# A hybrid retention and attention block on one core: six units in the lead, and rotary units written out by hand before the values

## The chip, the cores and the metric

The kernel runs on one core of a Trainium2 chip, in one launch, and computes the whole block for 256 tokens. The metric is the device time of one execution in microseconds (us). For the kernel before there are three runs, of 1586.11, 1587.36 and 1590.63 us, and one profiled execution of 1590.42 us.

## What is computed

The input `x` has 256 tokens of width 2048. The part of the reference that the change touches is the projection of the tokens and what becomes of queries, keys and values of the retention branch:

```python
proj = u @ w_in                      # u = rmsnorm(x); w_in is 2048 x 11328
(r_q, r_k, r_v, r_g, c_q, c_kv, k_pe, g_ret, g_mla) = split(proj)
rq = rope(r_q as 8 heads of 128, positions)
rk = rope(r_k as 8 heads of 128, positions) * 128 ** -0.5
rv = r_v as 8 heads of 256
ry = groupnorm(retention(rq, rk, rv)) * silu(r_g)
merged = sigmoid(g_ret) * (ry @ w_ret_o) + sigmoid(g_mla) * (attention @ w_mla_o)
h = x + merged @ w_out;  h = h + relu(rmsnorm(h) @ w_up) ** 2 @ w_down
```

`rope(t)` gives `t * cos + swapped(t) * sin`, where the two halves of a head change places in `swapped` and `sin` carries the sign. All of it is in float32.

## The kernel before

**Precision.** Every product of float32 numbers is made from two parts, a high part and a low part (`hi`, `lo`). `split` (lines 543 to 551) makes them: ScalarE copies the value into `hi`, and VectorE subtracts to get `lo`. A weight block of 128x1024 numbers therefore costs one ScalarE cast (line 167 or 545) and one VectorE subtraction (line 168 or 546) before TensorE can use it.

**The buffers.** Weights land in `raw` tiles (a ring of five, 4 KB per partition each), and their parts go into rings of four `hi` and four `lo` tiles (`wtile`, lines 158 to 161). TensorE sums into eight banks: four in the pool `mm` and four in the pool `at`. All large tensors share six places of 16 KB per partition (`big`).

**Units.** Queries and keys are made in 16 units of 128 output channels, query and key of a head in turn. A unit takes 16 matmuls of 512 columns and 16 of 256 columns. Units 0 to 2 are made while `x` arrives: the lead (lines 582 to 615) loads blocks that hold 256 columns of transposed `x` and 3x128 weight columns for each of 16 steps of the contracted dimension, into three large tiles and with ten transfers of 316, 384, 640 and then mostly 1280 columns. Units 3 to 5 follow, with their own weight loads, beside the angle tables for the rotation (`angles`, `table`) and the mean square of `x` (`load_x`). Then a loop (lines 709 to 719) makes units 6 to 15; in each turn it joins the unit's two partial sums into an SBUF tile (`join`, lines 533 to 536) and rotates it (`rope`, lines 698 to 707: two multiplications on 64 partitions each, one on 128, and one addition), and until unit 11 it also rotates one early unit. At units 8 and 10 it makes combinations of `x` (`combine`, lines 222 to 237), with two `raw` tiles as working space.

**Products.** The values, and later the gate `gr`, the output product `yr` and the gate `gm`, go through `product` (lines 451 to 481). Each has two column halves of eight steps. Most steps are an `Eight` (two parts of 12 matmuls of 512 columns). In some, the `Seven`, seven products stand for eight; such a step has four parts of 6, 6, 6 and 3 matmuls, and its weights must first be combined on VectorE (lines 302, 311, 312). `SEVEN` says at which of the eight places they stand. A `Seven` uses seven banks, an `Eight` four. The four banks of the `Eight` lie in the pool `mm` in the first half and in `at` in the second, so the first `Seven` of a half needs banks that the half ahead of it still holds until its results have been read (`tokens`, line 725, and `gated`, on VectorE).

**Order.** Most of the kernel is put in order by a scheduler that works from a simulated timeline. The products stand in blocks with an order written by hand (`run`, `stream`, lines 425 to 449): part n is multiplied after the parts up to n+4 have been prepared and those up to n+6 loaded, and a list `later` holds work that is to follow some parts on. Instructions that the scheduler places may stand between those written by hand.

Of the kernel before, what the change touches and what calls it, by code (L numbers as in the profile page):

```python
# [25 lines left out]
RH = 8  # L26
# [34 lines left out]
N_VEC = 60  # L61
LEAD = S + 3 * P
LEAD_TILES = (0, 6, 12)
LEAD_CHUNKS = (0, 1, 2, 4, 6, 8, 10, 12, 14, 16)
C_ID, C_MASK = 0, 128
# [39 lines left out]
def block_kernel(ctx: ExitStack, tc: tile.TileContext, A):  # L105
# [86 lines left out]

    def lora_pair(src, x):
        hi, lo = weights(src, [P, 2, LT, P])
        ps = mmps(f"lt{uid[0]}")
        for i in range(2):
            out = ps[:, i * S : (i + 1) * S]
            for k in range(LT):
                PE.matmul(out, hi[:, i, k], x.hi(k), start=k == 0, stop=False)
                PE.matmul(out, hi[:, i, k], x.lo(k), start=False, stop=False)  # L200
            for k in range(LT):
                PE.matmul(out, lo[:, i, k], x.hi(k), start=False, stop=k == LT - 1)
            yield i, out

# [16 lines left out]

    def combine(pair, j, o):
        n = o.shape[1]
        x, q = wtile("raw", [P, n, 2, 2, P]), wtile("raw", [P, n, 4, P])
# [12 lines left out]
        yield  # L237
        split(o[:, :, 0], o[:, :, 1], q)
# [136 lines left out]
    class Eight:  # L375
# [33 lines left out]
        def after(self, part):  # L409
            pass  # L410
# [170 lines left out]

    lead = [act.tile([P, 4096], F32, tag="act16", name=f"lead{i}") for i in range(3)]
    vec0 = lead[0][:, :N_VEC]
    x = Pair("x")
    posi = ip.tile([P, S], I32, name="posi")
    firsts = [mmps(f"first{j}") for j in range(3)]

    def lead_at(k):
        i = sum(k >= b for b in LEAD_TILES[1:])
        return lead[i], (N_VEC if i == 0 else 0) + (k - LEAD_TILES[i]) * LEAD  # L590

    def lead_x(k):
        t, o = lead_at(k)
        return t[:, o : o + S]

    for k0, k1 in zip(LEAD_CHUNKS, LEAD_CHUNKS[1:]):
        n = k1 - k0
        t, o = lead_at(k0)
        d = N_VEC + k0 * LEAD
        skip = N_VEC if k0 == 0 else 0  # L600
        cuts = (-skip, S, LEAD) if k0 == 0 else (0, n * LEAD)
        for c0, c1 in zip(cuts, cuts[1:]):
            tc.keep_in_program_order(
                nc.sync.dma_start(t[:, o + c0 : o + c1], A["lead"][:, d + c0 : d + c1])
            )
        blk = t[:, o : o + n * LEAD].rearrange("p (k c) -> p k c", c=LEAD)
        for k in range(k0, k1):
            split(x.hi(k), x.lo(k), lead_x(k), scale=vec0[:, V_MIX + k : V_MIX + k + 1])
        hi, lo = (wtile(kind, [P, n, 3 * P]) for kind in ("hi", "lo"))
        split(hi, lo, blk[:, :, S:])  # L610
        for j, ps in enumerate(firsts):
            w = hi[:, :, j * P : (j + 1) * P], lo[:, :, j * P : (j + 1) * P]
            t_pass1(ps, w, x, k0, n, k0 == 0)
            t_pass2(ps, w, x, k0, n, k1 == KT)

# [17 lines left out]

    early = ip.tile([P, 6, S], F32, name="early")
    for j in range(3):
        join(early[:, j], firsts[j])
    con = cp.tile([P, N_CONST], F32, name="con")
    tc.keep_in_program_order(nc.sync.dma_start(con, A["con"]))
    ident = con[:, C_ID : C_ID + P]
    mask = con[:, C_MASK : C_MASK + 384]  # L640

# [3 lines left out]

    firsts.append(mmps("first3"))
    t_half(firsts[3], A["w_rqk"][3], x, 0)
    t_half(firsts[3], A["w_rqk"][3], x, 1)
    tc.keep_in_program_order(nc.sync.dma_start(posi, A["positions"].partition_broadcast(P)))
    V.tensor_copy(posf, posi)  # L650
    join(early[:, 3], firsts[3])
    angles(0)
    xn = ip.tile([P, 2, D], F32, name="xn")
    ssx = ip.tile([P, 2], F32, name="ssx")

    def load_x(t):
        tc.keep_in_program_order(nc.sync.dma_start(xn[:, t], A["x"][t * P : (t + 1) * P]))
        SC.activation(xn[:, t], xn[:, t], AF.Square, accum_out=ssx[:, t : t + 1])

    load_x(0)  # L660
    lates = mmps("first4")
    t_unit(lates, A["w_rqk"][4], x)
    join(early[:, 4], lates)
    load_x(1)
    angles(1)
    lates = mmps("first5")
    t_unit(lates, A["w_rqk"][5], x)
    join(early[:, 5], lates)
    rx = cp.tile([P, 2], F32, name="rx")
# [29 lines left out]
    def rope(out, ps, cos, sin, step):  # L699
        tmp = rope_pool.tile([P, S], F32, tag="rope", name="rope")  # L700
        for d in range(0, P, step):
            s = d + step if (d // step) % 2 == 0 else d - step
            V.tensor_tensor(
                out=tmp[d : d + step], in0=ps[s : s + step], in1=sin[s : s + step], op=ALU.mult
            )
        V.tensor_tensor(out=out, in0=ps, in1=cos, op=ALU.mult)  # L706
        V.tensor_tensor(out=out, in0=out, in1=tmp, op=ALU.add)

    qk = big("qk", shape=(P, 2, RH, S))
    for u in range(6, 2 * RH):  # L710
        if u in (8, 10):
            for _ in combine(x, u - 8, xc[:, u - 8 : u - 6 if u == 8 else 3]):
                pass
        ps = mmps(f"qk{u}")
        t_unit(ps, A["w_rqk"][u], x)
        if u < 12:
            rope(qk[:, u % 2, u // 2 - 3], early[:, u - 6], *tabs[0], 64)
        rope(qk[:, u % 2, u // 2], joined(ps), *tabs[0], 64)
    ictx.close()

    rv = big("rv", shape=(P, 2, D))
    def tokens(out, act):
# [149 lines left out]
    def after(n):  # L872
        nonlocal making
        if n == 20:
            making = combine(ry, 0, yc[:, :2])
        elif n == 32 and yc.shape[1] > 2:
            making = combine(ry, 2, yc[:, 2:])
        if n % 2 == 0:
            next(making, None)
# [4 lines left out]
    with ExitStack() as mctx:  # L884
# [5 lines left out]
        def lora_norm(s, parts):  # L890
            n = len(parts) // 2
            cn = lpool.tile([P, 2, LORA], F32, name=f"cn{s}")
            ss = lpool.tile([P, 2, n], F32, name=f"ss{s}")
            for i, (t, c0, ps) in enumerate(parts):
# [3 lines left out]
                )  # L898
            r = lpool.tile([P, 2], F32, name=f"rc{s}")
            if n == 1:  # L900
# [38 lines left out]
        def late_turn():  # L939
            for _ in lora_turn(1, cn):  # L940
                pass
            pk = atps("pk")
            for t in range(2):
                PE.transpose(pk[:, t * P : (t + 1) * P], kn[:, t].rearrange("p j n -> p (j n)"), ident)
            rope(kpe, pk[:, :S], *tabs[1], 32)

# [31 lines left out]
        def mla_scores(h):  # L978
# [8 lines left out]
            pr = mp.tile([P, 384], F32, tag="pr", bufs=3, name=f"pr{h}")  # L987
            mx = mp.tile([P, 4], F32, tag="mx", bufs=4, name=f"mx{h}")
            parts = (slice(0, P), slice(P, 384))
# [44 lines left out]
        def mla_projections(g):  # L1034
            j0 = 2 * (g % 2)
            for i, ps in lora_pair(A["w_qpe"][g // 2, :, j0 : j0 + 2], cq):
                pe = mp.tile([P, S], F32, tag="pe", bufs=3, name=f"pe{g}{i}")
                rope(pe, ps, *tabs[1], 32)
                pes = vkp[:, 5 + g % 2, i * S : (i + 1) * S].rearrange("p (j n) -> p j n", j=2)
                split(pes[:, 0], pes[:, 1], pe[:, P:])  # L1040
                heads[2 * g + i, "pe"] = pe, pes
                yield
# [497 lines left out]
```

## Time and profile before

| | us |
|---|---|
| median of three runs | 1587.36 |
| the profiled execution | 1590.42 |
| its span, first to last instruction | 1588.7 |
| TensorE busy in the span | 1568.5 |
| VectorE busy | 1307.8 |
| ScalarE busy | 953.9 |

The span is what the views below divide up. The execution's own time is 1.7 us longer than the span. A matmul counts as busy from its start until its modelled end, and matmuls overlap, so a busy TensorE is not yet one at its peak; the distance between the starts of two matmuls says how fast it goes. The granted clock is given as a share of full speed: 1.00 is 2.4 GHz, and the other level, 0.50, is 1.2 GHz.

### The profile page before, as it was taken

The page shows a single profiled execution, that of the slowest core. Times are in us where ns is not written, and L with a number is a line of the kernel's source. Part 1 is how long each engine was busy: PE and PEld are TensorE (multiplying, and loading weights), DVE is VectorE, ACT ScalarE, POOL GpSimd, SP SyncE. Part 2 cuts the span into 40 slices and gives each one's busy share as a digit, 9 for nine tenths or more (in the row PEclk, how much of TensorE's full clock was granted, in tenths as well). Part 3 has the DMA queues.
Part 4 walks back from the last instruction along what each step waited for, and adds up shares of the span by engine and source line. Part 5 has one row for each costly group of instructions (what it writes and reads, how often), then busy time and mean ns, then how long its engine had stood idle before and what let it go on. Part 6 is the DMA issues. An engine that isn't in the chain of part 4 may idle for free.

```text
span 1588.7 us, 21686 instructions
## 1 busy us (share of the span) xinstructions
PE 1568.5 (99%) x7831; PEld 1326.2 (83%) x7831; DVE 1307.8 (82%) x1797; ACT 953.9 (60%) x1398; POOL 40.8 (3%) x75
## 2 busy tenths in 40 slices
PE   8999999999999999999999999999999999999997
PEld 7878888887888889888888888888888888888886
DVE  7999777798976988774667598888877899999996
ACT  6546555465545557765345576666676766666664
POOL 0000000000000000000000000000010100000000
PEclk9999999999999999999999999999999999999999
DMA  8566654455656664444564666667576977686773
GB/s 319 178 208 204 214 174 161 157 196 189 211 164 222 208 202 133 133 133 142 188 227 157 237 236 214 211 230 239 200 234 208 356 268 248 239 311 223 263 254 113
DMA packets 107195, 333.72 MB, mean 210 GB/s; under 512 B 11216, under 2 KB 11856, under 8 KB 106064
## 3 DMA queue, kind: packets, MB, share of 16 engines
q1 hardware_dynamic: 103776, 318.71, 59.8%
q0 software_dynamic: 3168, 11.54, 1.8%
q10 hardware_dynamic: 144, 2.10, 0.4%
q8 instruction: 61, 1.00, 0.3%
q14 instruction: 46, 0.38, 0.1%
HBM read 319.72 MB, written 12.58 MB: 209 GB/s over the span
## 4 chain that ended last, share of the span: by engine, by line
PE 75%; DVE 4%; issue 1%; DMA 1%; ACT 0%; DVEq 0%; POOLq 0%; POOL 0%; ACTq 0%
PE z L175 9%; PE dn L352 7%; PE dn L354 7%; PE dn L353 7%; PE z L179 5%; PE zs L328 2%; PE zs L329 2%; PE zs L330 2%; PE mo L215 2%; PE mo L216 2%; PE mo L218 2%; PE wo L216 2%; PE wo L215 2%; PE wo L218 2%; PE gm L354 2%; PE gm L352 2%
## 5 line engine op out<-in xcount | busy, mean ns | idle before, releaser
L168 DVE TENSOR_TENSOR lo<-raw,hi 128x1024 fp32r<-128x1024 f32 (+1 forms) x174 | 204.8, 1179 | 94.9 <-ACT hi L167 91.9
L167 ACT CAST hi<-raw 128x1024 fp32r<-128x1024 f32 (+1 forms) x174 | 175.9, 1017 | 176.2 <-PE mo L216 48.1
L546 DVE TENSOR_TENSOR lo<-raw,hi 128x1024 fp32r<-128x1024 f32 (+1 forms) x181 | 198.2, 1110 | 19.2 <-ACT hi L545 18.2
L545 ACT CAST hi<-raw 128x1024 fp32r<-128x1024 f32 (+1 forms) x181 | 171.0, 962 | 52.5 <-PE rg L216 6.1
L546 DVE TENSOR_TENSOR morelo<-raw,morehi 128x1024 fp32r<-128x1024 f32 (+1 forms) x131 | 141.7, 1102 | 21.8 <-ACT morehi L545 19.7
L545 ACT CAST morehi<-raw 128x1024 fp32r<-128x1024 f32 (+1 forms) x131 | 121.7, 952 | 22.1 <-DVE qk L706 6.0
L545 ACT CAST hi<-forms 128x1024 fp32r<-128x1024 f32 x70 | 73.7, 1053 | 50.7 <-DVE forms L302 27.6
L175 PE MATMUL z<-hT,morehi 128*128 128x512 f32 x408 | 101.6, 391 | 0.0
L352 PE MATMUL dn<-hi,dd 128*128 128x512 f32 x230 | 89.6, 389 | 0.0
L354 PE MATMUL dn<-hi,dd 128*128 128x512 f32 x230 | 89.5, 389 | 0.0
L353 PE MATMUL dn<-lo,dd 128*128 128x512 f32 x230 | 89.5, 389 | 0.0
L546 DVE TENSOR_TENSOR lo<-forms,hi 128x1024 fp32r<-128x1024 f32 x70 | 85.0, 1220 | 5.3 <-ACT hi L545 4.9
L175 PEld LDWEIGHTS z<-hT,morehi 128*128 128x128 f32 x408 | 74.9, 188 | 14.4
L1215 ACT COPY hs<-z 128x512 f32<-128x512 f32 x40 | 23.5, 587 | 72.3 <-PE z L179 72.3
L352 PE MATMUL dn<-morehi,dd 128*128 128x512 f32 x156 | 60.7, 389 | 0.0
L353 PE MATMUL dn<-morelo,dd 128*128 128x512 f32 x156 | 60.7, 389 | 0.0
L354 PE MATMUL dn<-morehi,dd 128*128 128x512 f32 x156 | 60.7, 389 | 0.0
L179 PEld LDWEIGHTS z<-hT,morelo 128*128 128x128 f32 x408 | 55.7, 190 | 4.0
L175 PE MATMUL z<-hT,hi 128*128 128x512 f32 x232 | 57.9, 392 | 0.0
L179 PE MATMUL z<-hT,morelo 128*128 128x256 f32 x408 | 56.9, 282 | 0.0
L302 DVE TENSOR_TENSOR forms<-raw,sraw 128x1024 f32<-128x1024 f32 x46 | 56.1, 1219 | 0.0
L215 PE MATMUL mo<-hi,my 128*128 128x512 f32 x128 | 51.0, 401 | 0.0
(488 smaller groups left out, 4223.9 us busy)
## 6 DMA issues: line engine op xcount, KB each, us to landing
raw<-w_down SPq DMA_DIRECT2D x106, 512.0 KB, 6.0
raw<-w_up SPq DMA_DIRECT2D x80, 512.0 KB, 5.4
raw<-w_rv SPq DMA_DIRECT2D x32, 512.0 KB, 4.8
raw<-w_rg SPq DMA_DIRECT2D x32, 512.0 KB, 3.8
raw<-w_gret SPq DMA_DIRECT2D x32, 512.0 KB, 4.1
raw<-w_ret_o SPq DMA_DIRECT2D x32, 512.0 KB, 4.7
raw<-w_gmla SPq DMA_DIRECT2D x32, 512.0 KB, 4.3
raw<-w_mla_o SPq DMA_DIRECT2D x32, 512.0 KB, 3.6
```

What stands on the lines that cost most here:

```text
L167: SC.copy(hi, raw)
L168: V.tensor_tensor(out=lo, in0=raw, in1=hi.bitcast(F32), op=ALU.subtract)
L175: PE.matmul(out, w[0][:, k], x.both(k0 + k), start=start and k == 0, stop=False)
L179: PE.matmul(out[:, :S], w[1][:, k], x.hi(k0 + k), start=False, stop=stop and k == n - 1)
L215: PE.matmul(out, x.hi(k0 + k, ts), w[0][:, k], start=start and k == 0, stop=False)
L216: PE.matmul(out, x.lo(k0 + k, ts), w[0][:, k], start=False, stop=False)
L218: PE.matmul(out, x.hi(k0 + k, ts), w[1][:, k], start=False, stop=stop and k == nk - 1)
L352: PE.matmul(q, ah, wh, start=start, stop=False)
L353: PE.matmul(q, ah, wl, start=False, stop=False)
L354: PE.matmul(q, al, wh, start=False, stop=self.left[f] == 0)
L545: SC.copy(hi, val)
L546: V.tensor_tensor(out=lo, in0=val, in1=hi.bitcast(F32), op=ALU.subtract)
```

## The change

Five things are changed, without touching the number of matmuls or of weight bytes.

- The lead brings units 0 to 5 (`FIRSTS = 6`) and 1024 columns per step, in 16 steps, each through a `raw` tile except the first. Positions and constants are loaded after step 3, the rows of `x` after steps 7 and 11. Unit loads 3 to 5 vanish as such.
- Units 6 to 15 become `Turned` parts, two for each unit, and stand ahead of the values in one order written by hand.
- `rope` works on a query-key pair at once (256 columns twice in one instruction); the six early units are rotated after parts 7, 15 and 60.
- `combine` gets its own tiles, and the values' product gets its working tiles from `big` instead of from a pool that opens after the units' pool has closed; its spare ring is two pairs deep where it was three.
- The places of the `Seven` move from (1, 3, 5) to (2, 4, 5) in four second halves and in the first half of `yr`. Some small tiles become wider than what is used of them, and the rotation in the attention part also takes two at once.

```diff
-SEVEN = {"rv": ((2, 4, 5), (1, 3, 5)), "gr": ((3, 5), (1, 3, 5)), "yr": ((1, 3, 5), (1, 3, 5)), "gm": ((3, 5, 6), (1, 3, 5))}
+XC = 2, 10
+EARLIES = 7, 15, 60
+SEVEN = {"rv": ((2, 4, 5), (2, 4, 5)), "gr": ((3, 5), (2, 4, 5)), "yr": ((2, 4, 5), (2, 4, 5)), "gm": ((3, 5, 6), (2, 4, 5))}
...
-LEAD = S + 3 * P
+FIRSTS = 6
+LEAD = S + FIRSTS * P
...
-    def combine(pair, j, o):
+    def combine(pair, j, o, pool=None):
...
+    for k in range(KT):
+        t = lead0[:, N_VEC:] if k == 0 else wtile("raw", [P, LEAD])
+        d = N_VEC + k * LEAD
+        cuts = {0: (-N_VEC, S, S + 3 * P, LEAD), 1: (0, S + 3 * P, LEAD)}.get(k, (0, LEAD))
         for c0, c1 in zip(cuts, cuts[1:]):
...
+            fetch((lead0 if k == 0 else t)[:, o + c0 : o + c1], A["lead"][:, d + c0 : d + c1])
+        if k == 3:
+            fetch(posi, A["positions"].partition_broadcast(P))
+            fetch(con, A["con"])
+        elif k in (7, 11):
+            r = (k - 7) // 4
+            fetch(xn[:, r], A["x"][r * P : (r + 1) * P])
+            SC.activation(xn[:, r], xn[:, r], AF.Square, accum_out=ssx[:, r : r + 1])
+        split(x.hi(k), x.lo(k), t[:, :S], scale=vec0[:, V_MIX + k : V_MIX + k + 1])
+        hi, lo = (wtile(kind, [P, FIRSTS * P]) for kind in ("hi", "lo"))
+        step = 3 if k < 2 else FIRSTS
+        for j in range(0, FIRSTS, step):
+            cs = slice(j * P, (j + step) * P)
+            split(hi[:, cs], lo[:, cs], t[:, S:][:, cs])
+            for i in range(j, j + step):
+                PE.matmul(firsts[i], hi[:, i * P : (i + 1) * P], x.both(k), start=k == 0, stop=False)
+            for i in range(j, j + step):
+                PE.matmul(firsts[i][:, :S], lo[:, i * P : (i + 1) * P], x.hi(k), start=False, stop=k == KT - 1)
...
+        def mm(self, part):
...
+            t_pass1(self.ps, w, x, part * HK, HK, part == 0)
+            t_pass2(self.ps, w, x, part * HK, HK, part == 1)
+            if part:
...
+                join(vals[h][:, i], self.ps)
+                if i:
+                    later.append([1, lambda: rope(qk[:, :, h], vals.pop(h), *tabs[0], 64)])
...
-    kctx, kp, tmp = room("ka", 3, False)
-    run(product([], "rv", A["w_rv"], x, xc, tmp, SEVEN["rv"], tokens(rv, AF.Copy), range(KP)))
-    kctx.close()
+    spare = big("sparea", F32R, (P, 2, 2, 1024))
+    sums = big("sumsa", shape=(P, 8, 512))
+    tmp = sums[:, :4]
+    rings(None, 2, False, sums[:, 4:].rearrange("p (a b) n -> p a b n", a=2), spare)
+    parts = [(t, h) for t in map(Turned, range(FIRSTS, 2 * RH)) for h in range(2)]
...
+    run(product(parts, "rv", A["w_rv"], x, xc, tmp, SEVEN["rv"], tokens(rv, AF.Copy), range(KP)), after)
+    ictx.close()
```

## Rows read from the trace of the kernel before

**Rows 1.** The page's first part: busy time, share of the span and instructions of each engine.

```profile
PE 1568.5 (99%) x7831; PEld 1326.2 (83%) x7831; DVE 1307.8 (82%) x1797; ACT 953.9 (60%) x1398; POOL 40.8 (3%) x75
```

**Rows 2.** Busy time by stretches of 10 us: the stretch in us from the span's start, its length, busy us and instructions of TensorE (PE), weight load (PEld), VectorE (DVE), ScalarE (ACT) and GpSimd (POOL), then the granted clock, the DMA share and GB/s.

```profile
0.00:10.00 10.00, 5.76 (x20) 2.99 (x20) 2.48 (x6) 4.14 (x8) 0.71 (x8) 1.00 0.79 275
10.00:20.00 10.00, 9.08 (x42) 7.77 (x43) 9.76 (x18) 9.89 (x20) 0.00 (x0) 0.83 0.98 391
20.00:30.00 10.00, 10.00 (x61) 8.86 (x60) 7.78 (x19) 5.47 (x9) 0.00 (x0) 1.00 0.98 404
...
100.00:110.00 10.00, 7.19 (x26) 5.43 (x25) 9.85 (x17) 2.46 (x3) 0.00 (x0) 0.83 0.48 159
110.00:120.00 10.00, 10.00 (x46) 8.25 (x45) 9.94 (x11) 5.95 (x7) 0.00 (x0) 1.00 0.64 205
...
380.00:390.00 10.00, 6.69 (x27) 4.34 (x26) 9.93 (x14) 7.08 (x9) 0.00 (x0) 1.00 0.44 144
390.00:400.00 10.00, 10.00 (x46) 8.28 (x45) 9.73 (x11) 5.69 (x6) 0.00 (x0) 1.00 0.61 206
```

**Rows 3.** Who TensorE waited for, over the whole span: total us, times, longest us.

```profile
PE yr L352 <- DVE m L725: 3.2, 3, 2.2
PE first L175 <- ACT hi L545: 2.9, 1, 2.9
PE rv L352 <- DVE val L536: 2.8, 1, 2.8
...
PE first L175 <- DVE x L549: 1.0, 2, 0.8
```

**Rows 4.** The timeline of the start: start us, us, engine, line, operation, out<-in, count, and in brackets the idle time before it with what ended it.

```profile
3.44 0.51 ACT L548 ACTIVATE x<-lead 128x256 fp32r<-128x256 f32 x1 [1.21 <-DMA lead<-lead]
...
4.61 0.93 PE L175 MATMUL first<-x,hi 128*128 128x512 f32 x3 [0.23 <-DVE x L549]
...
5.38 0.52 PE L179 MATMUL first<-x,lo 128*128 128x256 f32 x3
...
5.51 0.51 ACT L548 ACTIVATE x<-lead 128x256 fp32r<-128x256 f32 x1 [1.09 <-DMA lead<-lead]
...
6.69 0.94 PE L175 MATMUL first<-x,hi 128*128 128x512 f32 x3 [0.79 <-DVE x L549]
...
9.24 0.91 ACT L548 ACTIVATE x<-lead 128x256 fp32r<-128x256 f32 x2 [2.81 <-DMA lead<-lead]
...
10.92 2.92 PE L175 MATMUL first<-x,hi 128*128 128x512 f32 x6 [2.95 <-ACT hi L545]
```

**Rows 5.** TensorE's timeline: the matmuls of one whole unit from 32.74 us on, the start of the next unit, and the first matmul of the values.

```profile
32.74 3.82 PE L175 MATMUL first<-x,hi 128*128 128x512 f32 x16
...
36.39 2.08 PE L179 MATMUL first<-x,lo 128*128 128x256 f32 x16
...
38.30 2.00 PE L175 MATMUL first<-x,hi 128*128 128x512 f32 x8
...
100.04 0.40 PE L352 MATMUL rv<-hi,x 128*128 128x512 f32 x1
```

**Rows 6.** The timeline around 105 us, where the values begin; columns as in Rows 4.

```profile
101.88 0.39 PE L354 MATMUL rv<-hi,x 128*128 128x512 f32 x1
...
102.00 1.22 DVE L546 TENSOR_TENSOR lo<-raw,hi 128x1024 fp32r<-128x1024 f32 x1
...
104.60 0.42 DVE L536 TENSOR_TENSOR val<-qk,join 128x256 f32<-128x256 f32 x1
...
105.07 0.50 PE L352 MATMUL rv<-hi,x 128*128 128x512 f32 x1 [2.81 <-DVE val L536]
...
108.12 0.63 PE L352 MATMUL rv<-hi,x 128*128 128x512 f32 x1
```

**Rows 7.** TensorE's and VectorE's rows around 384 us, in the first half of `yr`.

```profile
381.46 0.39 PE L354 MATMUL yr<-hi,ry 128*128 128x512 f32 x1
...
383.18 0.68 DVE L725 TENSOR_TENSOR m<-gr,kbsums 128x512 f32<-128x512 f32 x1
...
384.01 0.47 PE L352 MATMUL yr<-hi,ry 128*128 128x512 f32 x1 [2.16 <-DVE m L725]
...
386.85 0.50 PE L352 MATMUL yr<-hi,yc 128*128 128x512 f32 x1 [0.19 <-DVE m L725]
...
387.85 0.68 DVE L725 TENSOR_TENSOR m<-gr,kbsums 128x512 f32<-128x512 f32 x1
...
388.68 0.47 PE L352 MATMUL yr<-spare,yc 128*128 128x512 f32 x1 [0.86 <-DVE m L725]
```

**Rows 8.** Timeline rows of ScalarE and VectorE between 42 and 95 us: a combination's first operation, two multiplications of a rotation, two subtractions in a row, and at the end a cast for the values (line 545) ahead of a unit's join (line 535).

```profile
42.49 1.22 DVE L226 TENSOR_TENSOR raw<-x 128x1024 f32<-128x1024 f32 x1
...
46.73 1.28 ACT L689 ACT_TABLE_LOAD   x1
...
81.17 0.85 DVE L703 TENSOR_TENSOR rope<-val,sin 64x256 f32<-64x256 f32 x2
...
85.21 2.35 DVE L168 TENSOR_TENSOR lo<-raw,hi 128x1024 fp32r<-128x1024 f32 x2
...
90.95 1.06 ACT L545 CAST hi<-raw 128x1024 fp32r<-128x1024 f32 x1 [1.47 <-PE qk L175]
...
94.72 0.37 ACT L535 COPY join<-qk 128x256 f32<-128x256 f32 x1 [0.90 <-PE qk L179]
```

More of the change, by code (lines that the diff above doesn't have):

```diff
@@ L191, in t_unit, with lora_pair @@
             t_pass2(out, w, x, half * HK, HK, half == 1)
-    def lora_pair(src, x):
+    def lora_pair(src, x, whole=False):
         hi, lo = weights(src, [P, 2, LT, P])
@@ L202, in lora_pair @@
                 PE.matmul(out, lo[:, i, k], x.hi(k), start=False, stop=k == LT - 1)
-            yield i, out
+            yield i, out if not whole else ps
     def n_unit(outs, src, x, k0, nk, start, stop):
@@ L220, in block_kernel @@
     PRODUCTS = ((3, 0, 0), (4, 0, 1), (2, 1, 0), (5, 1, 1), (6, 2, 0), (1, 2, 1), (7, 3, 0))
-    def combine(pair, j, o):
+    def combine(pair, j, o, pool=None):
         n = o.shape[1]
-        x, q = wtile("raw", [P, n, 2, 2, P]), wtile("raw", [P, n, 4, P])
+        if pool:
+            x, q = (
+                pool.tile([P, n, 2, 2, P], F32, tag=f"mix{i}", bufs=1, name=f"mix{i}{uid[0]}_{j}") for i in range(2)
+            )
+            q = q.rearrange("p j k t n -> p j (k t) n")
+        else:
+            x, q = wtile("raw", [P, n, 2, 2, P]), wtile("raw", [P, n, 4, P])
         hi, lo = pair.span(2 * j, 2 * n)
@@ L580, in mm3 @@
         PE.matmul(out, sl, mh, start=False, stop=stop)
-    lead = [act.tile([P, 4096], F32, tag="act16", name=f"lead{i}") for i in range(3)]
-    vec0 = lead[0][:, :N_VEC]
+    lead0 = ip.tile([P, N_VEC + LEAD], F32, name="lead0")
+    vec0 = lead0[:, :N_VEC]
     x = Pair("x")
     posi = ip.tile([P, S], I32, name="posi")
[L586 to L601, printed above, removed]
-        for c0, c1 in zip(cuts, cuts[1:]):
[L603 to L614, printed above, removed]
+    xn = ip.tile([P, 2, D], F32, name="xn")
@@ L632, in angles @@
         angs.append((ang, kk))
[L634 to L640, printed above, removed]
+    V.tensor_copy(posf, posi)
+    angles(0)
+    angles(1)
     def rms(out, ss, n, width):
@@ L644, in rms @@
         G.tensor_tensor(out=out, in0=out, in1=negh[:, :width], op=ALU.pow)
[L646 to L668, printed above, removed]
+    early = ip.tile([P, FIRSTS, S], F32, name="early")
+    for j in range(FIRSTS):
+        join(early[:, j], firsts[j])
     rx = cp.tile([P, 2], F32, name="rx")
@@ L703, in rope, with __init__, load, prep @@
             V.tensor_tensor(
-                out=tmp[d : d + step], in0=ps[s : s + step], in1=sin[s : s + step], op=ALU.mult
+                out=tmp[d : d + step],
+                in0=ps[s : s + step],
+                in1=sin[s : s + step].to_broadcast([step, n, S]),
+                op=ALU.mult,
             )
-        V.tensor_tensor(out=out, in0=ps, in1=cos, op=ALU.mult)
+        V.tensor_tensor(out=out, in0=ps, in1=cos.to_broadcast([P, n, S]), op=ALU.mult)
         V.tensor_tensor(out=out, in0=out, in1=tmp, op=ALU.add)
     qk = big("qk", shape=(P, 2, RH, S))
[L710 to L719, printed above, removed]
+    class Turned:
+        def __init__(self, u):
+            self.u, self.raw, self.ws = u, {}, {}
+        def load(self, part):
+            self.raw[part] = wtile("raw", [P, HK, P])
+            nc.sync.dma_start(self.raw[part], A["w_rqk"][self.u][:, part * HK : (part + 1) * HK])
+        def prep(self, part):
+            hi, lo = pair([P, HK, P])
+            split(hi, lo, self.raw.pop(part))
+            self.ws[part] = hi, lo
+        def mm(self, part):
+            if part == 0:
+                self.ps = atps(f"qk{self.u}")
+            w = self.ws.pop(part)
+            t_pass1(self.ps, w, x, part * HK, HK, part == 0)
+            t_pass2(self.ps, w, x, part * HK, HK, part == 1)
+            if part:
+                h, i = divmod(self.u, 2)
+                if i == 0:
+                    vals[h] = rope_pool.tile([P, 2, S], F32, tag="val", bufs=2, name=f"val{h}")
+                join(vals[h][:, i], self.ps)
+                if i:
+                    later.append([1, lambda: rope(qk[:, :, h], vals.pop(h), *tabs[0], 64)])
+    vals = {}
     rv = big("rv", shape=(P, 2, D))
@@ L741, in room, with after @@
         return ctx, pool, tmp
-    kctx, kp, tmp = room("ka", 3, False)
-    run(product([], "rv", A["w_rv"], x, xc, tmp, SEVEN["rv"], tokens(rv, AF.Copy), range(KP)))
-    kctx.close()
+    spare = big("sparea", F32R, (P, 2, 2, 1024))
[3 more added lines that the diff above has]
+    parts = [(t, h) for t in map(Turned, range(FIRSTS, 2 * RH)) for h in range(2)]
+    making = iter([])
+    def after(n):
+        nonlocal making
+        if n in XC:
+            i = 2 * XC.index(n)
+            making = combine(x, i, xc[:, i : min(i + 2, 3)], ip)
+        next(making, None)
+        if n in EARLIES:
+            h = EARLIES.index(n)
+            rope(qk[:, :, h], early[:, 2 * h : 2 * h + 2], *tabs[0], 64)
+    run(product(parts, "rv", A["w_rv"], x, xc, tmp, SEVEN["rv"], tokens(rv, AF.Copy), range(KP)), after)
+    ictx.close()
     ry = Pair("ry")
@@ L1035, in mla_projections @@
             j0 = 2 * (g % 2)
[L1036 to L1041, printed above, removed]
+            for i, ps in lora_pair(A["w_qpe"][g // 2, :, j0 : j0 + 2], cq, True):
+                if i:
+                    pe = mp.tile([P, 2, S], F32, tag="pe", bufs=2, name=f"pe{g}")
+                    rope(pe, ps.rearrange("p (i n) -> p i n", i=2), *tabs[1], 32)
+                    pes = vkp[:, 5 + g % 2].rearrange("p (i j n) -> p i j n", i=2, j=2)
+                    split(pes[:, :, 0], pes[:, :, 1], pe[:, :, P:])
+                    for n in range(2):
+                        heads[2 * g + n, "pe"] = pe[:, n], pes[:, n]
                 yield
```

30 lines of the change are left out of this document (20 added, 10 removed).

## The prediction

> **What bounds the kernel now.** I read the page's busy times first. TensorE works in 1568.5 us of a span of 1588.7 [rows 1], and the change leaves the number of matmuls and their shapes as they are. So at most the 20 us in which TensorE stands still can be won, and beside them the stretches in which it runs at the lower of its two clock levels, which count as busy. The second view, busy time by stretches of 10 us, shows where these are [rows 2]: between 0 and 20 us, between 100 and 110, between 380 and 390 and at the very end; in the other rows shown TensorE is busy for the full 10.00. The third, the table of waits, names them [rows 3]: `yr` waits 3.2 us for VectorE's `m` at line 725, the first units 2.9 us for a cast and 1.0 for `x`, the values 2.8 us for a join at line 536. What the change is worth is the sum over these places, less what it makes new. The kernel's end, after the last matmul, is not touched.
>
> **Start of the values.** At 101.88 us TensorE starts the last matmul it can, and the next comes at 105.07 [rows 6]. Matmuls of 512 columns follow each other every 0.23 us (3.65 us from the first to the second pass of 16 [rows 5]), so 3.0 us are lost. VectorE is what is late: it is busy for 9.85 of the 10 us [rows 2] and does two subtractions of 1.22 us ahead of the last unit's join at 104.60 [rows 6]. The bank that this join reads is the one that the values wait for. Shortly after, matmuls take 0.63 us where they took 0.39 [rows 6], and the granted clock of the stretch is 0.83 [rows 2]: 3.4 us at 0.50, the 1.2 GHz level, which cost another 1.7. Both sum to **4.7 us**.
>
> In the new order the last unit's parts are 18 and 19, and the first `Seven` of the values stands behind four parts of an `Eight`, 12 matmuls or 2.7 us each. The units now use the pool `at`, the first `Eight` uses `mm`, so no bank is wanted at once, and the last join has 11 us. Whether VectorE keeps up: in a unit's 5.56 us [rows 5] TensorE does two parts, so the 20 parts last 55.6. VectorE has 20 subtractions at 1.18 (two take 2.35 [rows 8]), 23.5; 10 joins at 0.42 [rows 6], 4.2; four instructions for each paired rotation at the 0.68 that 512 columns cost [rows 7], seven of them in this time, 19.0; the combinations, six operations for two sets at once (two at 1.22 [rows 8], four at 0.42, 4.1) and six for the third alone (two at 0.68, four of 128 columns at most at 0.42, 3.0), 7.1; six joins of early units, 2.5. That is 56 us, as much as TensorE needs, and with four parts, 11 us, prepared ahead there is a reserve. Before, eight pairs were rotated at 2 x 4 x 0.42, 3.4 us each; paired they take 2.7 (two multiplications of 64 partitions take 0.85 [rows 8]). The 5 us saved are VectorE's and count only by keeping the reserve. I take all 4.7; the bounds are nothing, if VectorE begins this stretch 11 us behind, and 4.7, since there is no more than that to win here.
>
> **Start of `yr`.** TensorE stops after 381.46 and goes on at 384.01, 386.85 and 388.68, each time when VectorE has read one more bank at line 725, from 383.18 to 387.85 [rows 7]. The stretch has 6.69 us of work in 10 [rows 2], and each of four breaks hides the 0.16 us by which a modelled matmul (0.39) overlaps the next: 3.3 + 0.6 = **3.9 us**. With the first `Seven` at place 2, two more parts or 5.5 us come first, and TensorE asks for these banks from about 387.2 on, one after another until about 390. VectorE frees them from 383.9 to 388.5. I take all 3.9. Bounds: nothing if the second `Eight`'s preparation pushes the four readings back by the same 5.5 us, and 3.9. The other second halves have no wait today [rows 3], so their later first `Seven` is worth nothing; what could suffer is under the rivals.
>
> **The lead.** TensorE starts at 4.61 us and needs 5.56 us per unit [rows 5], 89.0 for 16. The values start at 100.04 [rows 5], so the start loses at most 6.5 us; the idle times 0.79 and 2.95 [rows 4] and 1.7 for the clock of 0.83 from 10 to 20 us [rows 2] make 5.4. I take 6.0. The cause is visible: 316 columns of the lead have landed at 3.44, 1340 at 5.51 and 2620 only at 9.24 [rows 4], and three units want only 1.04 us of TensorE per step.
>
> With six units a step gives 2.08 us of work. The second three units of step 0 need 1084 columns, by interpolation at 5.0 us, a little before TensorE is through with the first three at 5.9. Step 1 needs 1724 columns: interpolated at 6.6; at the earliest at 6.0 (384 columns or 0.2 MB at 404 GB/s [rows 2]); at the latest at 8.1, if the whole delay of the piece that landed at 9.24 lies ahead of them. From landing to matmul are 1.2 us (3.44 to 4.61 [rows 4]), and step 0 keeps TensorE until about 7.1. So it stands still for 0.1, 0.7 or 2.2 us. I take 2.2, since the only transfer that landed in that stretch was late. With 0.4 for the smaller edges the start loses 2.6 instead of 6.0, a gain of **3.4 us**; the bounds are 1.7 less, if the clock falls all the same (it fell after 2.95 us of rest [rows 4] and stayed at 1.00 after 2.16 [rows 2, 7]), and 5.5. Afterwards a step's 0.5 MB needs 1.3 us at 391 GB/s [rows 2] against 2.08 of TensorE, ScalarE needs about 1.3 and VectorE 1.4 (0.5 for `x`, a bit under 1.0 for the weights). The loads of `x`'s rows, 1 MB after steps 7 and 11, are 2.7 us of transfer each and fall into a surplus of 0.8 us per step.
>
> **Costed at nothing.** The combinations' own tiles, the wider small tiles, and the paired rotation in the attention part, which lies in stretches where TensorE never waits [rows 3]. If that cover were gone, each would give or cost below 1 us. The spare ring of two pairs in place of three: part n+4 then waits for part n-2, still four parts ahead.
>
> **Sum.** 4.7 + 3.9 + 3.4 = 12.0 us off the profiled execution, from 1590.4 to 1578.4. The median of the runs stands 3.1 us lower and the runs spread over 4.5 us, so it may lack one of the two slow-clock stretches (1.7). I subtract 12.0 less 1.7 from 1587.4: **1577 us**.
>
> **The rivals.**
>
> *Only part of it.* The lead gains nothing, or one of the two waits comes back in the new place because VectorE's readings are pushed back: 12.0 less 3.4 to 4.7, so 1579 to 1582. For it speaks that VectorE is above 9.7 in 10 at each place [rows 2].
>
> *A new wait at the end of the lead.* If the parts written by hand come after the joins of six units and the tables on ScalarE, TensorE waits for six joins (0.37 each), a table load (1.28), four table operations (about 0.5), a cast and a subtraction (1.06 and 1.18 [rows 8]), 7.7 us, and 1.7 of slow clock: 12.0 less 9.4, 1585 us, no change that can be told. Against it: casts for the values, in an order written by hand, stand at 90.95 ahead of a unit's join at 94.72 [rows 8], so the scheduler mixes.
>
> *Two `Seven` in a row.* At places 4 and 5 VectorE needs for each 1.22 + 2 x 0.68 for the forms and 3 x 1.18 + 0.68 for the low parts, 6.8 us, against 21 matmuls or 4.8 us; two in a row make 4.0 us of delay. It decides where the parts ahead don't cover it, and in five halves would cost 20 us: 1597, slower. Against it: the values' first half already has (2, 4, 5), and no row of the waits shows it [rows 3]. Same place, a fixed order: it could also be smaller and only eat the gain.
>
> *The lead becomes a matter of transfers.* If each 0.5 MB came as slowly as the piece that ended at 9.24 (0.66 MB in 3.73 us [rows 4], so 3.0 us a step), 16 steps would take 48 us against 33, and the lead's gain would turn into a loss of 14: 1593, slower. It decides where a step takes longer than 2.08 us. Against it: 391 and 404 GB/s from 10 to 30 us, with pieces of 0.66 MB [rows 2]. The Trainium skill, "DMA: Bandwidth & Descriptors", section "Measured (HBM→SBUF, 128 partitions, SWDGE, issued from GpSimd)", asks for transfers of at least 1 MiB; by the fit on that page, 2.0 us and 436 GB/s, a step's transfer takes an estimated 3.2 us, which is this rival. By that rule the trace does not go, since transfers of 0.66 MB already run one into another there.
>
> **How the numbers follow.** Forecast 0.56, only part of it 0.22, the lead's end 0.12, two `Seven` 0.06, transfers 0.04. The range takes the forecast with the lead's upper bound (14.1 off, 1573) and most of the third case: 1573 to 1585. A measurement of this kernel can tell 0.3%, 4.8 us, from no change. The first two cases lie beyond it but for a few: faster 0.77; the lead's end and small losses: same 0.14; slower 0.09.
>
> **What would show it.** Right: no wait of the values for a join, none of `yr` for line 725, TensorE full from about 12 us on, and a granted clock of 1.00 from 100 to 110. The values should begin at about 96.5. A gap of TensorE near 41 us would show the lead's end; waits of `rv`, `gr`, `yr` or `gm` for a subtraction at the lines of `split`, the two `Seven`; a gap in every step until 50 us, the transfers. The prediction is wrong if TensorE's idle time outside the end of the kernel is still above 8 us.

## The result, and the profile after

The kernel after takes 1578.78 us (median of 4 runs, 1578.56 to 1579.15), the kernel before 1586.79 beside it; the ratio is 0.9945, with an interval of 0.9928 to 0.9962. That is 8.0 us less where 10.4 were forecast (1577, in a range of 1573 to 1585), and clear of the 0.3% that can be told.

The profiled execution of after has a span of 1576.8 us against 1588.7. These 11.9 us agree with the prediction's sum of 12.0, but that says little: the execution of before that the sum was made from was one of the longest, and one term of the sum is not in most executions. The runs of after lie within 0.6 us of each other, those of before spread over 4.5.

The stretches that answer to [rows 2], in the kernel after (start and end, length, busy us of PE, PEld, DVE, ACT and POOL, granted clock, DMA share, GB/s):

```profile
0.00:10.00 10.00, 7.97 (x33) 4.97 (x34) 4.18 (x9) 6.01 (x12) 0.71 (x8) 1.00 0.72 229
10.00:20.00 10.00, 9.82 (x54) 8.10 (x53) 9.21 (x22) 6.07 (x11) 0.00 (x0) 1.00 1.01 410
20.00:30.00 10.00, 9.62 (x54) 8.09 (x53) 10.00 (x25) 8.71 (x14) 0.00 (x0) 1.00 1.00 388
...
100.00:110.00 10.00, 10.00 (x46) 8.26 (x45) 9.45 (x12) 4.75 (x6) 0.00 (x0) 1.00 0.45 142
...
380.00:390.00 10.00, 10.00 (x45) 8.28 (x45) 8.97 (x10) 5.54 (x6) 0.00 (x0) 1.00 0.63 201
```

And what TensorE still waits for in the whole span, against [rows 3]:

```profile
PE spin L575 <- DVE cold L572: 1.2, 1, 1.2
PE first L624 <- DVE x L556: 0.8, 1, 0.8
PE first L624 <- ACT hi L552: 0.4, 1, 0.4
```

The waits of the values and of `yr` are gone, and the clock stays at 1.00 from 100 to 110 us. But look at the counts between 10 and 30 us: TensorE does 54 matmuls per 10 us, where a full stretch of such steps has 60 or so [rows 2]. It is busy by the column and yet slower; the lead did not become what the prediction said. Of the prediction's own signs, TensorE's idle time outside the end of the kernel is 2.7 us where more than 8 would have been wrong, but the values begin at 97.3 us instead of 96.5, and TensorE is not full from 12 us on.

To see such small losses, I add up for each profile by how much the starts of successive matmuls lie further apart than usual (0.2275 us after 512 columns, 0.1195 after 256, 0.131 after 288, 0.05 after 128). The table has this loss in us for three stretches, beside the median of all runs of each kernel. The first stretch begins with the lead's first matmul, which starts between 4.25 and 4.86 us; a value below zero means starts a little closer than usual. "Elsewhere" is what a variant loses more than the kernel it was made from: "to 200" from 110 to 200 us, "after 400" from 400 to 600. The experiments follow below; "before" and "after" are the profiles shown. In the groups of runs that the variants come from, the kernel before had medians from 1587.02 to 1587.41.

| kernel | 4 to 45 | 45 to 110 | 310 to 400 | elsewhere | median |
|---|---|---|---|---|---|
| before | 6.2 | 4.9 | 4.1 | | 1586.79 |
| before once more | 3.1 | 4.9 | 3.4 | | 1586.76 |
| after | 3.7 | 0.3 | -0.3 | | 1578.78 |
| after once more | 4.1 | 0.3 | -0.3 | | 1578.84 |
| before, `yr` places | 3.4 | 4.9 | -0.3 | 1.9 after 400 | 1585.68 |
| before, own tiles | 2.3 | 6.2 | 0.5 | | 1583.34 |
| after, units by the scheduler | 5.0 | 3.0 | -0.3 | | 1584.64 |
| after, single rotations | 4.3 | 1.3 | -0.3 | 2.0 to 200 | 1581.45 |
| after, old places | 3.5 | 0.3 | -0.2 | 1.1 after 400 | 1581.26 |
| after, raw tiles | 3.5 | 0.3 | 1.5 | | 1580.92 |
| after, old lead | 5.9 | 0.3 | -0.3 | | 1578.24 |
| after, angles late | 3.3 | 1.7 | -0.3 | 0.5 to 200 | 1581.42 |
| after, angles and squares late | 4.5 | 2.4 | -0.3 | | 1581.56 |
| after, positions later | 2.2 | 0.3 | -0.3 | | 1578.48 |

### The profile page after: what moved, and what is told of

The parts are those of the page before. It is cut to its first block, busy times and chain, and to the rows that moved or that the text cites. A ratio compares the mean times of both kernels' runs of the same rounds, so it can differ in the third digit from the quotient of the medians.

```text
span 1576.8 us, 21649 instructions
## 1 busy us (share of the span) xinstructions
PE 1565.1 (99%) x7831; PEld 1325.1 (84%) x7831; DVE 1301.3 (83%) x1740; ACT 951.7 (60%) x1397; POOL 38.9 (2%) x75
## 4 chain that ended last, share of the span: by engine, by line
PE 81%; issue 0%; ACT 0%; DVE 0%; DVEq 0%; POOLq 0%; POOL 0%; ACTq 0%
PE z L176 9%; PE dn L360 7%; PE dn L361 7%; PE dn L359 7%; PE z L180 5%; PE zs L335 2%; PE zs L336 2%; PE zs L337 2%; PE mo L216 2%; PE mo L217 2%; PE mo L219 2%; PE wo L216 2%; PE wo L217 2%; PE wo L219 2%; PE gm L359 2%; PE yr L360 2%
## 5 line engine op out<-in xcount | busy, mean ns | idle before, releaser
L169 DVE TENSOR_TENSOR lo<-raw,hi 128x1024 fp32r<-128x1024 f32 (+1 forms) x148 | 173.3, 1172 | 96.3 <-ACT hi L168 96.1
L553 DVE TENSOR_TENSOR lo<-raw,hi 128x1024 fp32r<-128x1024 f32 (+3 forms) x214 | 231.9, 1101 | 24.9 <-ACT hi L552 23.4
L168 ACT CAST hi<-raw 128x1024 fp32r<-128x1024 f32 (+1 forms) x148 | 149.5, 1011 | 160.1 <-PE mo L217 47.2
L552 ACT CAST hi<-raw 128x1024 fp32r<-128x1024 f32 (+3 forms) x214 | 200.1, 954 | 53.7 <-issue 7.8
L553 DVE TENSOR_TENSOR morelo<-raw,morehi 128x1024 fp32r<-128x1024 f32 (+1 forms) x118 | 127.1, 1098 | 17.6 <-ACT morehi L552 17.1
L552 ACT CAST morehi<-raw 128x1024 fp32r<-128x1024 f32 (+1 forms) x118 | 109.1, 950 | 10.2 <-issue 3.2
```

What stands on the lines that cost most here:

```text
L168: SC.copy(hi, raw)
L169: V.tensor_tensor(out=lo, in0=raw, in1=hi.bitcast(F32), op=ALU.subtract)
L552: SC.copy(hi, val)
L553: V.tensor_tensor(out=lo, in0=val, in1=hi.bitcast(F32), op=ALU.subtract)
```

## The experiments

**What a run of before loses.** The file is unchanged.

> The kernel before, unchanged, profiled once more. Theory: the three places of idle time (start, values, yr) are in every execution, about 3.7, 3.0 and 3.3 us of them by the busy column, but the two stretches at the 1.2 GHz clock level (1.7 us each) are not; the profiled execution of 1590.42 us had both, so one near 1586.5 us should show one of them or none, and the change is then worth 12.0 less 3.4 = 8.6 us against such executions. Rival: idle and clock are the same in every execution, the span is 1588.7 us again, and the 3.5 us between the runs lie elsewhere. The ratio should be 1.000 either way.

Ratio 0.9996 (0.9985 to 1.0007), median 1586.76 over 11 runs from 1585.23 to 1590.45. The profiled execution is one of 1586.76 us. Its start and its stretch around 100 us:

```profile
7.57 0.91 ACT L548 ACTIVATE x<-lead 128x256 fp32r<-128x256 f32 x2 [1.37 <-DMA lead<-lead]
```

```profile
9.26 1.65 PE L175 MATMUL first<-x,hi 128*128 128x512 f32 x6 [1.30 <-ACT hi L545]
```

```profile
10.00:20.00 10.00, 10.00 (x59) 8.72 (x59) 10.00 (x19) 9.61 (x18) 0.00 (x0) 1.00 1.02 402
...
100.00:110.00 10.00, 7.87 (x28) 6.38 (x29) 9.89 (x15) 4.30 (x5) 0.00 (x0) 0.83 0.46 143
```

The transfer for steps 2 and 3 is there at 7.57 us instead of 9.24 [rows 4], TensorE rests for 1.30 us instead of 2.95, and the clock stays at 1.00 from 10 to 20 us. The loss in the first 45 us is 3.1 us instead of 6.2. The slow stretch at 100 us is in both profiles. So the theory holds for one of the two slow stretches: that of the start came in one profile and not in the other, together with the late arrival of one transfer.

**Places of the `Seven`, alone.** Of the line of `SEVEN`, only the entry that changes is shown:

```diff
-"yr": ((1, 3, 5), (1, 3, 5))
+"yr": ((2, 4, 5), (1, 3, 5))
```

> The kernel before with one tuple changed: yr's first half has its Sevens at (2, 4, 5) instead of (1, 3, 5). Theory: the three waits of yr for line 725 go (3.2 us in the table of waits, 3.9 us with the overlaps), nothing else moves, 3.9 us faster, about 1582.9 us. Rival: the two added Eight parts push the readings at line 725 back, the wait only moves, and the time stays at 1586.8 us.

Ratio 0.9987 (0.9978 to 0.9996), some 2 us of the 3.9. The waits for line 725 go from this half, but two others appear in the table of waits:

```profile
PE yr L352 <- DVE kbsums L866: 0.9, 1, 0.9
...
PE gm L352 <- DVE gm L725: 0.3, 1, 0.3
```

They stand at 423 us, where the second half of `yr` still has its first `Seven` at place 1, and at 557 us. About half of the gain came, the other half moved on.

**The combinations' own tiles, alone.** The kernel before, with the tiles for `ry` taken from the product's own pool (and `combine` with the parameter for it):

```diff
-            making = combine(ry, 0, yc[:, :2])
+            making = combine(ry, 0, yc[:, :2], kp)
...
-            making = combine(ry, 2, yc[:, 2:])
+            making = combine(ry, 2, yc[:, 2:], kp)
```

> The kernel before with one thing changed: the combinations of ry get tiles of their own instead of two of the five raw tiles; places as before. Theory: it is the occupied raw tiles that make loads of gr late (VectorE stands 2.1 us for a transfer at 356 us) and VectorE late for line 725, so the waits of yr (2.5 to 3.2 us) fall to below 1 us: 2 to 3.5 us faster than 1587.0. Rival, the prediction's step: only later places end the wait, and the time does not change.

Ratio 0.9973 (0.9960 to 0.9986): 2 to 6 us faster, with the old places. The stretch of `yr` in this kernel is full, and of the waits in these products one of 0.6 us is left, in `gr`:

```profile
380.00:390.00 10.00, 10.00 (x46) 8.29 (x45) 9.90 (x12) 6.82 (x8) 0.00 (x0) 1.00 0.66 212
```

```profile
PE gr L358 <- DVE m L731: 0.6, 1, 0.6
```

The 6.2 us of its profile from 45 to 110 us, more than before, come with more slow clock around the rest at the values (2.80 us): the granted clock of the row is 0.66 where before has 0.83:

```profile
100.00:110.00 10.00, 8.63 (x25) 6.84 (x26) 9.89 (x15) 4.61 (x5) 0.00 (x0) 0.66 0.50 158
```

The reason for the gain can be read in the kernel before, in VectorE's timeline ahead of the wait: with two of the five `raw` tiles held by a combination, the loads of `gr` come late, and VectorE stands still for one before it falls behind.

```profile
356.32 1.23 DVE L302 TENSOR_TENSOR kbforms<-raw,raw 128x1024 f32<-128x1024 f32 x1 [2.10 <-DMA raw<-w_gret]
```

Two more rests of VectorE follow, 1.64 us before 369.6 and 2.07 before 372.9, for casts of ScalarE that had themselves waited 3.99 and 2.25 us for loads. From 330 to 385 us VectorE waits 6.0 us in all; with the tiles of their own it waits 0.6.

**Each of the two taken out of the kernel after.** The old places in all four products:

```diff
-SEVEN = {"rv": ((2, 4, 5), (2, 4, 5)), "gr": ((3, 5), (2, 4, 5)), "yr": ((2, 4, 5), (2, 4, 5)), "gm": ((3, 5, 6), (2, 4, 5))}
+SEVEN = {"rv": ((2, 4, 5), (1, 3, 5)), "gr": ((3, 5), (1, 3, 5)), "yr": ((1, 3, 5), (1, 3, 5)), "gm": ((3, 5, 6), (1, 3, 5))}
```

> The kernel after with all the Sevens at their old places. Theory: the waits of yr for line 725 come back, 3.9 us, so about 1582.7 us, and the other three products show no wait at either set of places. Rival: the own tiles of the combinations relieve VectorE there, and the time stays within 1 us of 1578.8 us.

Median 1581.26, 2.5 us slower than after (1.6 by the ratios, 0.9955 against 0.9945), but `yr` has no wait: the rival was right on that. The loss is a wait of `gm` at 550 us (1.1 us by the table) and a longer end, 10.5 instead of 9.4 us from the last matmul to the last instruction. The difference lies behind the last operation of any engine, which ends 4.7 us after the last matmul's start in both; why it is there stays open.

And the combinations, of `x` and of `ry`, in `raw` tiles again (the calls of `combine` without their last argument):

> The kernel after with the combinations of x and of ry again in raw tiles (two of the five). Theory: with new places and the order written by hand, own tiles are a reserve; a later load costs VectorE 2 us of waiting for transfers in gr, and yr's later Sevens cover it: within 1 us of the kernel after. Rival: the own tiles are what removed the wait of yr (with them and the old places there was none), and it comes back with 2 to 4 us.

Median 1580.92, 2.1 us slower, between the two theories; TensorE loses 1.8 us more than in after from 310 to 400 us, in `gr` this time:

```profile
PE gr L360 <- DVE spare L553: 0.8, 1, 0.8
```

In this kernel VectorE reads the four banks of `gr` as late as in before, counted from the first matmul of `yr`: the last reading starts 12.6 us behind it, where before has 11.6. But `yr` has no wait. First the two rows of before, then the two of this kernel:

```profile
376.25 0.39 PE L352 MATMUL yr<-hi,ry 128*128 128x512 f32 x1
...
L725 DVE TENSOR_TENSOR m<-gr,kbsums x4: 684/684/685, 383.2 to 387.8; 128x512 f32<-128x512 f32 x4
```

```profile
370.13 0.39 PE L359 MATMUL yr<-hi,ry 128*128 128x512 f32 x1
...
L736 DVE TENSOR_TENSOR m<-gr,kbsums x4: 682/685/686, 375.0 to 382.7; 128x512 f32<-128x512 f32 x4
```

So either of the two alone ends the wait of `yr`: the later places let TensorE ask later, the tiles let VectorE read earlier (in the kernel before with own tiles the last reading starts 6.6 us behind the first matmul). What is lost without one of them, about 2 us, is lost at other places.

**The order written by hand.** In the kernel after, units 6 to 15 go back into the scheduler's loop, with single rotations, the combinations of `x` in `raw` tiles, sums in the pool `mm` and the values' own pool:

```diff
+    for u in range(FIRSTS, 2 * RH):
...
+        t_unit(ps, A["w_rqk"][u], x)
...
-    parts = [(t, h) for t in map(Turned, range(FIRSTS, 2 * RH)) for h in range(2)]
...
+    kctx, kp, tmp = room("ka", 3, False)
+    run(product([], "rv", A["w_rv"], x, xc, tmp, SEVEN["rv"], tokens(rv, AF.Copy), range(KP)))
```

> The kernel after with its lead and its places, but units 6 to 15 again in the loop that the scheduler places, single rotations, combinations in raw tiles and the values' product with its own pool. Theory: the order written by hand is what removes the wait at the start of the values; it comes back with about 2.8 us (4.5 if the clock falls behind it), so 1581.6 to 1583.3 us. Rival: the six-unit lead alone relieves VectorE, and the time stays within 1 us of 1578.8 us.

Median 1584.64, 5.9 us above after's (by the ratios to before, 0.9976 against 0.9945, 4.9). The wait of the values is back, and a second one appears at the lead's end, where the first units want a bank that a join has not read yet:

```profile
PE rv L359 <- DVE val L543: 2.5, 1, 2.5
PE qk L176 <- DVE early L543: 1.2, 1, 1.2
```

The profiled execution, of 1582.68 us, is one of two short ones; the five others lie from 1584.51 to 1585.18 with a mean granted clock of 0.997 or 0.998 instead of 0.999. That would fit a slow clock behind the rest of the values, as the theory has it, but none of the five was profiled, so it is not shown. Several things went back at once. The `raw` tiles alone lose nothing from 45 to 110 us (0.3 in the row "after, raw tiles"); the next experiment takes the single rotations by themselves; the values' pool was not tried by itself.

**Paired rotations.** The order written by hand stays, each pair is rotated by two calls:

```diff
-                    later.append([1, lambda: rope(qk[:, :, h], vals.pop(h), *tabs[0], 64)])
+                    later.append([1, lambda: both(qk[:, :, h], vals.pop(h))])
...
+    def both(out, ps):
+        for i in range(2):
+            rope(out[:, i : i + 1], ps[:, i : i + 1], *tabs[0], 64)
```

> The kernel after with every rotation of the retention branch done singly again (four instructions of 256 columns for each unit, at the same places in the order). Theory: VectorE has no reserve from 60 to 130 us (with 8 us of angle work put there, 2.6 us were lost), so the 5 us that pairing saves are needed: rv waits for subtractions, 1.5 to 3 us slower than the kernel after, 1580.3 to 1581.8 us. Rival: the four parts prepared ahead cover 5 us, and the time stays within 0.5 us.

Median 1581.45, 2.6 us slower: the theory. The waits end at 101.69 and 112.93 us, in the values, and both are for subtractions:

```profile
PE rv L360 <- DVE lo L553: 2.1, 2, 1.4
```

```profile
101.69 0.50 PE L360 MATMUL rv<-lo,x 128*128 128x512 f32 x1 [0.72 <-DVE lo L553]
...
104.16 0.42 DVE L543 TENSOR_TENSOR val<-qk,join 128x256 f32<-128x256 f32 x1
```

The second row is the join of the last unit. It starts 6.3 us behind the first matmul of the values, where before has 4.6 (104.60 against 100.04 [rows 5, 6]) and the kernel after 0.9; and no matmul waits for it, since the units' sums now lie in the pool `at`. With the other pool a late join stops nobody, then; the paired rotations are needed for the subtractions. What the order adds by itself was not tried.

**The lead.** The old lead and units 3 to 5 as before, put into the kernel after in place of the new one:

```diff
-LEAD = S + FIRSTS * P
+LEAD = S + 3 * P
+LEAD_TILES = (0, 6, 12)
+LEAD_CHUNKS = (0, 1, 2, 4, 6, 8, 10, 12, 14, 16)
...
-    lead0 = ip.tile([P, N_VEC + LEAD], F32, name="lead0")
+    lead = [act.tile([P, 4096], F32, tag="act16", name=f"lead{i}") for i in range(3)]
```

> The kernel after with the lead of the kernel before (three units, ten transfers, units 3 to 5 loaded apart and placed by the scheduler); the units from 6 on and all else as after. It isolates the prediction's term for the lead, 3.4 us. By that term, 1582.2 us. Theory after the profiles: the old lead loses 3.1 to 6.2 us in 45 us and the new one 3.5 to 4.1, so the median is 0 to 1 us slower, and what the new lead brings is that executions no longer differ by 4 us. A second rival: the units 3 to 5 end in joins that the first units wait for (as with the old loop, 1.2 us), 1580 us.

Median 1578.24, half a us below the kernel after: as far as these runs can tell, the lead of six units is worth nothing in the median. The profiled execution was an untypical one of 1580.92 us, with the late transfer and the slow clock of the start; the others, but one of 1579.19, lie from 1577.93 to 1578.26. Its start has the row that [rows 4] has for before:

```profile
10.42 1.99 PE L178 MATMUL first<-x,hi 128*128 128x512 f32 x6 [2.72 <-ACT hi L554]
```

What holds the new lead back is in the timeline of after, steps 3 to 5:

```profile
11.36 0.30 DVE L646 CAST posf<-posi 128x256 f32<-128x256 int32 x1 [0.79 <-DMA posi<-positions]
...
11.56 0.48 DVE L556 SCALAR_TENSOR_TENSOR x<-raw,lead,x 128x256 fp32r<-128x256 f32 x1
...
12.19 1.63 PE L624 MATMUL first<-x,hi 128*128 128x512 f32 x6
...
13.34 0.51 ACT L555 ACTIVATE x<-raw,lead 128x256 fp32r<-128x256 f32 x1 [2.55 <-DMA raw<-lead]
...
14.63 1.65 PE L624 MATMUL first<-x,hi 128*128 128x512 f32 x6
```

VectorE waits for the positions before it may do step 3's `x`, and step 4's transfer comes behind positions and constants: steps 3 and 4 start 2.44 us apart where 2.12 would do. Three kernels test this. First, the kernel after with the angles pinned behind the lead:

```diff
-    V.tensor_copy(posf, posi)
+    tc.keep_in_program_order(V.tensor_copy(posf, posi))
```

> The kernel after with the angle computation pinned behind the lead's last subtraction on VectorE, by one added keep_in_program_order. Theory: in the lead of the kernel after, steps 2 to 7 take 2.2 to 2.4 us where 2.08 are needed, because the 8 us of angle work and the wait for the positions (0.79 us) stand ahead of the subtractions for x; moved behind the lead, the loss from 10 to 45 us falls from about 1.5 to 0.5 us, and the kernel is 1 us faster. Rival: the steps wait for transfers or for ScalarE, and nothing changes; or the 8 us come back as a wait at the first units written by hand, 1 to 3 us slower.

Median 1581.42, 2.6 us slower: from 15 us on the lead's steps do come every 2.12 us, and its loss after 20 us falls from 1.1 to 0.6; but VectorE's 8 us come back in the values, as the second rival said, with rests of 0.71 and 1.40 us of VectorE between 60 and 65 us for tables that ScalarE makes from the late angles:

```profile
110.00:120.00 10.00, 9.29 (x42) 7.45 (x41) 9.90 (x11) 3.87 (x5) 0.00 (x0) 1.00 0.56 176
```

With the squares of `x` pinned there as well (the same call around `SC.activation(... AF.Square ...)`, after the loop):

> As the kernel with late angles, and the two squares of x's rows (1.9 us each on ScalarE, each behind 1.2 us of waiting for its transfer) also pinned behind the lead. Theory: the wait of 0.4 us for a cast near 24 us goes too, 0.4 to 0.7 us faster than late angles alone. Rival: the squares, the power and the tables now end later than the first rotation wants them, and the first units wait, some us slower.

Median 1581.56. The rival again: two new waits, for what hangs on the squares.

```profile
PE qk L176 <- DVE rxb L668: 1.7, 1, 1.7
PE pb L666 <- DVE rr L663: 1.6, 1, 1.6
```

Last, with only the transfers moved:

```diff
-        if k == 3:
+        if k == 8:
...
-        elif k in (7, 11):
-            r = (k - 7) // 4
+        elif k in (10, 12):
+            r = (k - 10) // 2
```

> The kernel after with positions and constants loaded after step 8 of the lead instead of step 3, and the rows of x after steps 10 and 12 instead of 7 and 11. Theory: the transfers ahead of step 4 and the angle work that follows them make steps 2 to 7 slow; later, they fall where steps are already prepared ahead: the loss from 4 to 45 us falls from 3.7 to 4.1 us to 2.5 to 3, a kernel 0.7 to 1.5 us faster than the kernel after. Rival: the same work is only moved to steps 9 to 15, where it costs the same, or the tables come too late for the first rotation; no gain, or up to 2 us slower.

The stretch that was short of matmuls has 58 instead of 54:

```profile
10.00:20.00 10.00, 10.00 (x58) 8.76 (x57) 7.93 (x15) 7.03 (x12) 0.00 (x0) 1.00 0.91 324
```

The loss falls to 2.2 us in the profile, with a little of it moved to 33 us; but its first matmul of the lead starts at 4.86 us instead of 4.25. The median is 1578.48 and the ratio to before 0.9939 (0.9927 to 0.9951): 0.3 us below after, less than these runs can tell apart.

**The kernel after, once more.**

> The kernel after, unchanged, beside its variants and profiled once more. It shows how much its start and its three places vary between executions: theory, that only the first 10 us vary (arrival of the lead), by less than in the kernel before since no rest there is long enough to drop the clock; median 1578.5 to 1579.2 us. Rival: it varies over 4 us like the kernel before.

Median 1578.84, from 1578.60 to 1579.19. Against the expectation, the clock is not all that keeps it even: this profile rests at other places of the start (0.9 us before 12.7 us) and loses 4.1 us there.

## Why the prediction was right or wrong

**Start of the values: right, 4.7 us.** The loss is 4.9 us in both profiles of before and 0.3 in both of after, clock included. That no bank is wanted at once is borne out by the single rotations: the last join is as late as in before, and no matmul waits for it. The step's account of VectorE was too easy, though. I had 11 us of reserve and let the pairing of the rotations count for little; in fact the order by hand alone is not enough (single rotations: 2.6 us slower), and 8 us of angle work put into this stretch cost 2.6. The row of one paired multiplication agrees with the price I took (0.68):

```profile
L693 DVE TENSOR_TENSOR rope<-val,sin x10: 685/687/690, 58.6 to 103.0; 64x512 f32<-64x512 f32 x10
```

VectorE is above 9.8 in 10 from 60 to 100 us in the kernel after too; the reserve that keeps TensorE from waiting is below the 5 us or so that single rotations add to VectorE's work.

**Start of `yr`: the size and the step right, but only half of the story.** 3.4 to 4.1 us were lost there and none are now. The later places do what the prediction said: with the combinations in `raw` tiles the readings are as late as in before, and `yr` does not wait. But they are not the only thing that does it, and the prediction costed the own tiles at nothing, or below 1 us. The tiles alone ended the wait of `yr` too (ratio 0.9973), and taking them out of the kernel after costs 2.1 us, in `gr`; places alone brought 2 us and moved the rest. I had read who was late (VectorE at line 725), not why: a step further back, VectorE waits for loads that had no `raw` tile. In the kernel after that line, now 736, runs early; the four readings start from 0.7 to 8.4 us behind the first matmul of `yr` at 368.72, and no matmul waits for them:

```profile
L736 DVE TENSOR_TENSOR m<-gr,kbsums x4: 684/686/689, 369.4 to 377.1; 128x512 f32<-128x512 f32 x4
```

**The lead: wrong, the step that failed.** It gave 3.4 us, from 6.0 lost before and 2.6 after. Both were off. The 6.0 holds for executions with the late transfer and the slow clock (6.2 and 5.9 us in two profiles of the old lead); in the three others the start loses 2.3 to 3.4, in one of them since the transfer comes 1.7 us earlier and the clock does not fall. And the new lead loses 3.7 and 4.1 where I had 2.6. Of these, 1.6 and 1.3 are lost up to 10 us, within the 2.2 that I had taken for a late transfer; the term that was too small is the 0.4 for the smaller edges, which measured 2.1 and 2.9. I had looked at bytes per step and not at what stands in the queue ahead of a step (positions and constants ahead of step 4) or on VectorE (8 us of angle work, which are not in the prediction's 1.4 us per step). With the old lead the kernel after is as fast (1578.24 against 1578.78 and 1578.84).

**The sum.** 4.7 and 3.9 without a lead term are 8.6 us; measured were 8.0. The 1.7 us that the prediction took off because its profile was one of the longer executions were of the right kind but too small: the start alone loses 3.1 us more there than in the second profile of before. That the forecast of 1577 came within 2 us of the measured time is in part luck, since this 1.7 made up for half of the lead's 3.4. What else was costed at nothing (the spare ring, the wider small tiles, the rotation in the attention part) was not tried by itself.

**The rivals.** "Only part of it", with no gain in the lead, is what came, and its time of about 1579 is the one measured. No new wait at the lead's end arose, as the row at 90.95 [rows 8] had suggested; with the units left to the scheduler one did (1.2 us). Two `Seven` in a row show no wait in the profile of after. The lead did not become a matter of transfers: the stretch from 10 to 20 us moved 410 GB/s, in pieces of 0.5 MB. The Trainium skill, "DMA: Bandwidth & Descriptors", section "Measured (HBM→SBUF, 128 partitions, SWDGE, issued from GpSimd)", asks for transfers of 1 MiB or more, and measures them as issued from GpSimd. For these transfers, issued from SyncE, that row does not bear the rule out.

## What to carry to other kernels

When a wait ends in an engine that is late, follow that engine back one more step: a ring of load buffers that also serves as scratch can make VectorE late 25 us before TensorE notices. A profile is one execution; before a term is taken from its first 10 us, compare its time with the other runs, and take a slow-clock stretch as something that may be absent. Work moved into a stretch where VectorE has no room comes back: here 8 us of it cost 2.6. And when two changes aim at one wait, take each out alone: here either was enough for `yr`.

## What was not expected of the hardware

The arrival of the same transfer, in the same program, differed by 1.7 us between executions (9.24 and 7.57 us); the start lost 6.2 us in the one and 3.1 in the other, which is most of the 4.5 us by which the first runs of before differ (later ones went from 1584.86 to 1593.71). Why it arrives late at times was not tried. TensorE's clock fell to 0.50 with rests of 2.95 and 2.72 us at the start and 2.81 us at the values, and stayed at 1.00 with rests of 2.16 us in `yr` and, in one profile, 2.5 us at the values (the kernel with the units left to the scheduler).
